# Two-layer diffusion trunk with eight experts: another order of the experts, another order inside a weight block, one list of leftover blocks

## The chip, the cores and the metric

The kernel runs on one core of one Trainium2 chip. The metric is the device time of one execution in microseconds (us); lower is better.

## What is computed

The reference is a trunk of two layers over 256 tokens of width 1024 in fp32 (layer 0: mLSTM and differential attention, then a dense SwiGLU; layer 1: a convolution module, then eight experts). The change touches the last sub-layer alone, each token's top two of eight experts:

```python
logits = (tokens @ router_w).astype(F32)
top_vals, top_idx = lax.top_k(logits, TOP_K)          # TOP_K = 2 of N_EXPERTS = 8
gates = jax.nn.softmax(top_vals, axis=-1)
...
def run_block(args):                                   # D = 1024, D_FF_EXPERT = 2816
    tok_idx, e = args
    xb = tokens[tok_idx]
    return (jax.nn.silu(xb @ w1[e]) * (xb @ w3[e])) @ w2[e]
```

An expert's three matrices are 3 x 1024 x 2816 fp32 numbers, 34.6 MB; eight experts are 277 MB, read from HBM in every execution.

## The kernel before, in words

All weights lie in HBM in units of 128 x 2048 fp32, one 1 MB (1.05 million bytes) transfer each. An expert is 33 units: its hidden width 2816 is cut into blocks j = 0 to 5 (five of 512 columns, one of 256), and a 512-wide block has two units of w1 (h = 0, 1: the two halves of the 1024 contraction rows), two of w3 and two of w2; the last block has one of each. The m1 and m3 units of one (j, h) are the "unit pair" of the change.

**Slots.** At run time the tokens that chose an expert are counted and gathered into slots. Expert 0 has FIRST = 96 slots. The other seven are ranked by their counts, and the rank of an expert gives it `SLOTS` = 128, 96, 96, 96, 64, 64 or 32 slots. `TURNS` (L37) is the order in which expert 0 (None) and the ranks take their turns, so before it is, in slots: 96, 64, 96, 96, 32, 128, 96, 64. With the given inputs the counts are 60 for expert 0 and 98, 82, 78, 70, 55, 51, 18 by rank, so no token is left over.

**Two kinds of expert.** The 128-slot expert (class `Expert`) splits each weight half into a high and a low part on ScalarE and VectorE (`half`, L363) and runs three passes with the full array. An expert with fewer slots (`few`, class `Tiled`, L1835) multiplies fp32 weights as they land. Its slots are cut into 64 (`wide`, L1848: column tiles of 64, m1 and m3 side by side in the array) and 32 (`narrow`, L1851: column tiles of 32, four side by side); 96 slots use both, 64 only wide, 32 only narrow. The profile shows wide matmuls as 128*64 and narrow ones as 128*32; each fp32 matmul is two records. `up2` (L1857) does one unit pair: the wide matmuls of its contraction tiles, then its narrow ones. `down2` (L1897) does one m2 unit in the same way. `act` (L1870) is silu times gate on ScalarE and VectorE, `turn` and `turned` (L1881, L1891) transpose the result on TensorE and copy it on VectorE for `down2`.

**The order.** The list `todo` (L2149 to L2182) holds the products in TensorE's order: for block j the pairs of (j, 0) and (j, 1), then the m2 units of block j - 1. `later(n, ...)` hangs small work before the n-th next product: `act` at once, `turn` after `wait` further products (L2164). TensorE, VectorE and ScalarE keep the order as written (`in_order`). The gathers of the next group of experts (`GROUPS`, L38) are hung into blocks 2 and 3 of the expert before it, an expert's way back to its tokens (`back`) into the first block of the next one. At the start of expert 0, `ranks` (L1966) counts, ranks and prepares the leftover bookkeeping on GpSimd and VectorE; its VectorE instructions stand before the `act` of block 0.

**The transfers.** SyncE issues all weight transfers, in the order in which `todo` uses the units; each waits until the buffer it writes is free, and all behind it wait too. The list `room` (L1557 to L1564) says which buffers the units take in turn: 6 "raw", 4 "w" (the rings of high and low parts, where no expert splits), 1 "gp", 4 "B8", so 15 ahead; around the 128-slot expert, which needs the rings itself, 6 + 1 + 3 = 10. `whole` (L1558) is the place of the 128-slot expert in `TURNS`, and the list is cut by it: the cycles of 15 run up to 30 units before that expert, the cycles of 10 until 8 units behind it. Counted through the list, the last 11 units of the kernel before take three "w" buffers (253 to 255 of 0 to 263), three "B8" (256 to 258) and five "raw". "B8" has seven buffers; the output sum `acc` and the two parts of the tokens keep three, and the two parts of the sum (`sums_`, L2028) take two more from block 3 of the last expert on.

**Leftovers.** After the experts, `overflow` (L2043) would run experts again for tokens that found no slot: two numbers are loaded into registers of every engine, and two `If` blocks with a loop over all eight experts (`block`, L2055, written out in each) and a third `If` are passed. With these inputs all are jumped over.

Of the kernel before, what the change touches and what calls it, by code (L numbers as in the profile page):

```python
# [19 lines left out]
P = 128  # L20
# [13 lines left out]
FIRST = 96  # L34

SLOTS = (128, 96, 96, 96, 64, 64, 32)
TURNS = (None, 4, 1, 2, 6, 0, 3, 5)  # L37
GROUPS = ((0,), (1, 2), (3, 4), (5,), (6, 7))  # L38
NV = 2

# [196 lines left out]
def build(ctx: ExitStack, tc: tile.TileContext, d, unit, dbg=None):  # L237
# [1463 lines left out]
    def few(i):  # L1701
        return slots_of(i) < P
# [132 lines left out]
    class Tiled(Expert):  # L1835
# [21 lines left out]
        def up2(self, j, h, ws):  # L1857

            w_ = 512 if j < 5 else 256
            if h == 0:  # L1860
                self.pp = self.banks("mm")
            (x,), nk = self.x(), UW // w_
            for on, fn, o, s in ((self.A, self.wide, self.oa, 64), (self.B, self.narrow, self.ob, 32)):
                for k in range(nk if on else 0):
                    kk = nk * h + k
                    for n, w in enumerate(ws):
                        w = w[k // (nk // 2)].rearrange("p (k c) -> p k c", c=w_)[:, k % (nk // 2)]
                        fn(self.pp, x[:, kk, o : o + s], n, w, kk == 0, kk == KT - 1)

        def act(self, j):  # L1870
            w_ = 512 if j < 5 else 256
# [25 lines left out]
        def down2(self, j, h, w):  # L1897

            nf = 4 if j < 5 else 2
            if self.yp is None:  # L1900
                self.yp = self.banks("aux")
            t = self.hhl[j]
            for on, fn, o, s in ((self.A, self.wide, 0, 64), (self.B, self.narrow, 64 * nf * self.A, 32)):
                for k in range(2 if on else 0):
                    q = 2 * h + k
                    m = 64 * q if s == 64 else 64 * (q % (nf // 2)) + 32 * (q // (nf // 2))
                    for c in range(2):
                        fn(self.yp, t[:, o + m : o + m + s], c, w[k][:, 512 * c : 512 * c + 512], j + q == 0, j == 5 and q == 1)

        def parts(self, g=None):  # L1910

# [38 lines left out]
    bases = tl([P, NE - 1], "bases", I32)  # L1950

    posv, selv, gtv = (tl([P, TT, 2 * NE], n) for n in ("posv", "selv", "gtv"))
    cmi = tl([P, 2], "cmi", I32)

    def by_rank(dst, src):

# [9 lines left out]
    def ranks():  # L1966

        pcnt = pm("aux")
        for t in range(TT):
            mm(pcnt[:, 0:8], one, sel[:, t, :], t == 0, t == TT - 1)  # L1970
        cnt, key = tl([P, NE], "cnt"), tl([P, NE], "key")
        A.copy(cnt, pcnt[:, 0:8])

        G.tensor_scalar(key, cnt, float(NE), None, ALU.mult)
        G.tensor_tensor(key, key, K("iota8"), ALU.subtract)
        sq = [P, NE - 1, NE - 1]
        V.tensor_tensor(r7[0], key[:, 1:].unsqueeze(1).to_broadcast(sq), key[:, 1:].unsqueeze(2).to_broadcast(sq), ALU.is_gt)
        rank = tl([P, NE - 1], "rank")
        V.tensor_reduce(rank, r7[0], AX.X, ALU.add)
        i7 = K("iota8")[:, : NE - 1]  # L1980
        V.tensor_tensor(r7[1], rank.unsqueeze(1).to_broadcast(sq), i7.unsqueeze(2).to_broadcast(sq), ALU.is_equal)
        x = tl(sq, "r7", bufs=4)
        G.tensor_tensor(x, r7[1], K("iota8")[:, 1:].unsqueeze(1).to_broadcast(sq), ALU.mult)
        b = tl([P, NE - 1], "bf")
        V.tensor_reduce(b, x, AX.X, ALU.add)
        V.tensor_scalar(bases, b, float(NU), None, ALU.mult)
        by_rank(posr, pos)
        by_rank(selr, sel)

        cap = tl([P, NE], "cap")  # L1990
        G.memset(cap, float(FIRST))
        G.memset(cap[:, 1:], float(P))
        for r in range(1, NE - 1):
            if SLOTS[r] != SLOTS[r - 1]:
                x = tl([P, NE - 1], "capx", bufs=2)
                V.tensor_scalar(x, rank, float(r), float(SLOTS[r - 1] - SLOTS[r]), ALU.is_ge, ALU.mult)
                G.tensor_tensor(cap[:, 1:], cap[:, 1:], x, ALU.subtract)
        for n in range(2):
            c = slice(NE * n, NE * n + NE)
            for t in range(TT):  # L2000
                if n == 0:
                    G.tensor_tensor(posv[:, t, c], pos[:, t], cap, ALU.subtract)
                G.tensor_copy(selv[:, t, c], sel[:, t])
                G.tensor_copy(gtv[:, t, c], gt[:, t])
            G.tensor_tensor(cnt, cnt, cap, ALU.subtract)
            V.tensor_reduce(key[:, n : n + 1], cnt, AX.X, ALU.max)
            if n == 0:
                G.memset(cap, float(P))
        for t in range(TT):
            G.tensor_tensor(posv[:, t, NE:], posv[:, t, :NE], cap, ALU.subtract)  # L2010
        V.tensor_scalar(cmi, key[:, 0:2], 0.0, None, ALU.max)

    base = []

# [26 lines left out]
        return d["w"][bass.ds(base + unit[key], 1)].rearrange("o p c -> p (o c)")  # L2041

    def overflow():  # L2043
        over = [nc.values_load(cmi[0:1, n : n + 1], min_val=0, max_val=T) for n in range(2)]

        for n in range(2):
            with tc.If(over[n] > 0):  # L2047
                with tc.For_i(0, NE, 1) as e:
                    block(e, e + NE * n)
        with tc.If(over[0] > 0):  # L2050
            for t in range(TT):
                for c in range(2):
                    acc_parts(t, c)

    def block(e, q):  # L2055

        colv = tl([P, 3, TT], "ovc")
        for n, src in enumerate((posv, selv, gtv)):
# [10 lines left out]
        gather([O2[:, t, :] for t in range(TT)], [(0, P, g2)], bank="mm")  # L2069

        def load(n, j, h):
            return halves(raw(None, unit_from(e * NU, (n, 0, j, h))))

        x2 = Expert(lambda: g2, lambda w: OT2, lambda t: colv[:, 2, t : t + 1], bank="mm")
        for j in range(6):
# [73 lines left out]
    for i in range(NE):  # L2149
# [6 lines left out]
        for j in range(6):  # L2156
            for h in range(2 if j < 5 else 1):
                if few(i):
                    todo.append(([("m1", i, j, h), ("m3", i, j, h)], None, partial(x.up2, j, h)))
                else:  # L2160
                    for n in ("m1", "m3"):
                        for q in range(2):
                            todo.append(([(n, i, j, h)], q, partial(x.up, j, h, int(n == "m3"), q)))
            wait = 1 if few(i) else 2 if (i, j) == (last, 5) else 3  # L2164
            later(0, partial(x.act, j))
            later(wait, partial(x.turn, j), partial(x.turned, j))
            if (i, j) == (last, 1):
                later(2, row)
            if (i, j) == (last, 3):
                later(1, slot_gate, *[partial(acc_parts, t, c) for t in range(TT) for c in range(2)])  # L2170
            g = group_of.get(i + 1)
            if g is not None and g != group_of[i]:
                if j == 2:
                    later(0, partial(new_group, g), *[lambda g=g, t=t: groups[g].onehot(t) for t in range(TT)])
                    later(3, lambda g=g: groups[g].turn())
                if j == 3:
                    later(1, *[lambda g=g, k=k: groups[g].gather((k,)) for k in range(4)])
            if j:
                downs(i, j - 1)
            elif i:  # L2180
                downs(i - 1, 5)
# [104 lines left out]
```

## Time and profile before

| | us |
|---|---|
| median of 3 runs | 1334.69 (1329.05 to 1337.04) |
| the profiled execution | 1333.75 |
| its span, first to last instruction | 1331.9 |
| TensorE busy in the span | 1262.3 |
| expert 0 starts / the last product of the last expert ends | 603.0 / 1310.0 |
| units of weights read by the experts | 264 |

Times of rows are counted from the start of the span; what lies around the span is 1.85 us. "PE" is TensorE, "PEld" its weight loads, "DVE" VectorE, "ACT" ScalarE, "POOL" GpSimd, "SP" SyncE. A name with q (SPq, PEldq) is the engine's sequencer, which handles branches, semaphores and the issuing of transfers. The granted clock is 1.00 at 2.4 GHz and 0.50 at 1.2 GHz; a figure between is a mean over the stretch. A busy TensorE isn't one at its peak: the records of matmuls that run side by side overlap.

### The profile page before, as it was taken

The page shows a single profiled execution, that of the slowest core. Times are in us where ns is not written, and L with a number is a line of the kernel's source. Part 1 is how long each engine was busy: PE and PEld are TensorE (multiplying, and loading weights), DVE is VectorE, ACT ScalarE, POOL GpSimd, SP SyncE. Part 2 cuts the span into 40 slices and gives each one's busy share as a digit, 9 for nine tenths or more (in the row PEclk, how much of TensorE's full clock was granted, in tenths as well). Part 3 has the DMA queues.
Part 4 walks back from the last instruction along what each step waited for, and adds up shares of the span by engine and source line. Part 5 has one row for each costly group of instructions (what it writes and reads, how often), then busy time and mean ns, then how long its engine had stood idle before and what let it go on. Part 6 is the DMA issues. An engine that isn't in the chain of part 4 may idle for free. (4 is left out here: it accounts for less than half of the span.)

```text
span 1331.9 us, 22705 instructions
## 1 busy us (share of the span) xinstructions
PE 1262.3 (95%) x9256; PEld 799.1 (60%) x9256; DVE 630.6 (47%) x1040; ACT 430.3 (32%) x785; POOL 31.3 (2%) x78
## 2 busy tenths in 40 slices
PE   7999999899999998999999999999986999999994
PEld 5878777799998886684343333433443778434332
DVE  4689758698877667752101112011121888211122
ACT  4553346564434553342020000210002678100111
POOL 1000001100000000001000000000000000000000
PEclk9999999999999998888999999999999999999997
DMA  8728820478987626788789999998989999799963
GB/s 334 288 100 297 310 91 25 163 319 345 375 315 293 221 104 175 236 306 318 265 331 399 418 418 416 414 380 323 369 339 420 420 419 362 305 417 381 407 252 138
DMA packets 70808, 406.48 MB, mean 305 GB/s; under 512 B 7842, under 2 KB 12194, under 8 KB 31268
## 3 DMA queue, kind: packets, MB, share of 16 engines
q1 hardware_dynamic: 70692, 404.91, 78.6%
q8 instruction: 76, 1.25, 0.4%
q14 instruction: 40, 0.33, 0.1%
HBM read 402.94 MB, written 1.93 MB: 304 GB/s over the span
## 5 line engine op out<-in xcount | busy, mean ns | idle before, releaser
L373 DVE TENSOR_TENSOR wlo<-raw,whi 128x1024 fp32r<-128x1024 f32 x150 | 180.9, 1223 | 51.5 <-ACT whi L372 51.0
L282 PE MATMUL mm<-raw,gL 128*32 128x256 f32 (+3 forms) x1432 | 193.8, 441 | 7.9 <-DMA raw<-w 6.3
L372 ACT CAST whi<-raw 128x1024 fp32r<-128x1024 f32 x150 | 154.9, 1051 | 92.4 <-PE mm L282 59.1
L282 PE MATMUL mm<-B,whi 128*128 128x256 f32 x960 | 169.8, 280 | 0.2 <-DVE B L632 0.2
L1878 DVE TENSOR_TENSOR cv<-cv,mm 64x512 f32<-64x512 f32 (+1 forms) x36 | 23.3, 647 | 284.2 <-ACT cv L1877 283.9
L282 PEld LDWEIGHTS mm<-B,whi 128*128 128x128 f32 x960 | 147.5, 189 | 2.3 <-PE mm L282 0.6
L282 PEld LDWEIGHTS mm<-raw,gL 128*32 128x32 f32 (+1 forms) x1432 | 75.1, 121 | 105.6 <-issue 74.6
L282 PE MATMUL mm<-B,wlo 128*128 128x256 f32 x480 | 134.0, 279 | 0.0
L1877 ACT ACTIVATE cv<-mm 64x512 f32<-64x512 f32 (+1 forms) x36 | 19.9, 553 | 351.2 <-PE mm L282 351.1
L282 PE MATMUL mm<-B,gL 128*32 128x256 f32 (+3 forms) x736 | 112.0, 442 | 2.5 <-DMA B<-w 2.5
L282 PE MATMUL aux<-whi,pT 128*128 128x512 f32 (+2 forms) x392 | 104.1, 437 | 0.0
L282 PEld LDWEIGHTS mm<-B,wlo 128*128 128x128 f32 x480 | 90.4, 188 | 0.0
L282 PE MATMUL aux<-raw,pT 128*32 128x256 f32 (+1 forms) x632 | 79.0, 459 | 1.3 <-DVE cvt L1878 0.7
L282 PE MATMUL aux<-wlo,pT 128*128 128x512 f32 (+2 forms) x276 | 71.4, 442 | 1.1 <-DVE wlo L373 1.1
L282 PEld LDWEIGHTS mm<-B,gL 128*32 128x32 f32 (+1 forms) x736 | 41.5, 120 | 46.4 <-issue 33.8
L282 PEld LDWEIGHTS aux<-whi,pT 128*128 128x128 f32 (+2 forms) x392 | 49.0, 160 | 25.8 <-issue 14.7
L282 PE MATMUL mm<-U,whi 128*128 128x256 f32 (+1 forms) x240 | 64.3, 330 | 0.0
L282 PE MATMUL mm<-whi,B 128*128 128x512 f32 (+1 forms) x192 | 60.1, 389 | 2.9 <-ACT whi L372 2.9
L282 PE MATMUL aux<-B,pT 128*32 128x256 f32 (+2 forms) x392 | 58.6, 468 | 2.9 <-SPq L2047 2.9
L282 PE MATMUL mm<-whi,gL 128*32 128x256 f32 (+3 forms) x360 | 57.5, 443 | 0.0
L282 PE MATMUL mm<-wlo,gL 128*32 128x256 f32 (+3 forms) x360 | 56.2, 436 | 0.0
L282 PE MATMUL mm<-U,wlo 128*128 128x256 f32 (+1 forms) x160 | 52.4, 328 | 0.0
(454 smaller groups left out, 1836.5 us busy)
## 6 DMA issues: line engine op xcount, KB each, us to landing
raw<-w SPq DMA_DIRECT2D x239, 1024.0 KB, 7.3
B<-w SPq DMA_DIRECT2D x69, 1024.0 KB, 11.4
whi<-w SPq DMA_DIRECT2D x52, 512.0 KB, 8.5
wlo<-w SPq DMA_DIRECT2D x52, 512.0 KB, 9.0
gp<-w SPq DMA_DIRECT2D x16, 512.0 KB, 9.8
m<-w SPq DMA_DIRECT2D x16, 512.0 KB, 10.0
B<-hd SPq DMA_DIRECT2D x24, 142.0 KB, 5.2
x<-x SPq DMA_DIRECT2D x2, 512.0 KB, 4.7
```

The lines of the kernel that those rows point to most:

```text
L282: PE.matmul(out, lhsT, rhs, start=start, stop=stop)
L372: A.copy(hi, rq)
L373: V.tensor_tensor(lo, rq, f(hi), ALU.subtract)
L1877: A.activation(s, p_[:64, :w], AF.Silu)
L1878: V.tensor_tensor(s, s, p_[64:, :w], ALU.mult)
```

## The change

`TURNS` gives 96, 32, 96, 96, 64, 96, 128, 64 slots: the 32-slot expert comes second, the 128-slot expert seventh. `up2` and `down2` of an expert with both kinds of tiles run the wide matmuls of (j, 0) and of (j, 1) first and hold the narrow ones of both until then. `turn` of a few-slot expert comes one product later, but for block 0 of expert 0 and the last block of the last expert. `ranks` makes a list of at most eight leftover blocks (expert, place, count), and `overflow` runs one loop over that list under one `If`.

```diff
@@ -34,7 +34,7 @@
 FIRST = 96
 
 SLOTS = (128, 96, 96, 96, 64, 64, 32)
-TURNS = (None, 4, 1, 2, 6, 0, 3, 5)
+TURNS = (None, 6, 1, 2, 4, 3, 0, 5)
 GROUPS = ((0,), (1, 2), (3, 4), (5,), (6, 7))
 NV = 2
 
@@ -1858,14 +1858,23 @@
 
             w_ = 512 if j < 5 else 256
             if h == 0:
-                self.pp = self.banks("mm")
+                self.pp, self.held = self.banks("mm"), []
             (x,), nk = self.x(), UW // w_
-            for on, fn, o, s in ((self.A, self.wide, self.oa, 64), (self.B, self.narrow, self.ob, 32)):
-                for k in range(nk if on else 0):
-                    kk = nk * h + k
-                    for n, w in enumerate(ws):
-                        w = w[k // (nk // 2)].rearrange("p (k c) -> p k c", c=w_)[:, k % (nk // 2)]
-                        fn(self.pp, x[:, kk, o : o + s], n, w, kk == 0, kk == KT - 1)
+            ws = [[w[k // (nk // 2)].rearrange("p (k c) -> p k c", c=w_)[:, k % (nk // 2)] for w in ws] for k in range(nk)]
+
+            def go(fn, kk, w, o, s):
+                for n in range(2):
+                    fn(self.pp, x[:, kk, o : o + s], n, w[n], kk == 0, kk == KT - 1)
+
+            for k, w in enumerate(ws):
+                if self.A:
+                    go(self.wide, nk * h + k, w, self.oa, 64)
+                if self.B:
+                    self.held.append((nk * h + k, w))
+            if not self.A or nk * h + nk == KT:
+                for kk, w in self.held:
+                    go(self.narrow, kk, w, self.ob, 32)
+                self.held = []
 
         def act(self, j):
             w_ = 512 if j < 5 else 256
@@ -1899,13 +1908,24 @@
             nf = 4 if j < 5 else 2
             if self.yp is None:
                 self.yp = self.banks("aux")
-            t = self.hhl[j]
-            for on, fn, o, s in ((self.A, self.wide, 0, 64), (self.B, self.narrow, 64 * nf * self.A, 32)):
-                for k in range(2 if on else 0):
-                    q = 2 * h + k
-                    m = 64 * q if s == 64 else 64 * (q % (nf // 2)) + 32 * (q // (nf // 2))
-                    for c in range(2):
-                        fn(self.yp, t[:, o + m : o + m + s], c, w[k][:, 512 * c : 512 * c + 512], j + q == 0, j == 5 and q == 1)
+            if h == 0:
+                self.held = []
+            t, o = self.hhl[j], 64 * nf * self.A
+
+            def go(fn, q, w, m, s):
+                for c in range(2):
+                    fn(self.yp, t[:, m : m + s], c, w[:, 512 * c : 512 * c + 512], j + q == 0, j == 5 and q == 1)
+
+            for k in range(2):
+                q = 2 * h + k
+                if self.A:
+                    go(self.wide, q, w[k], 64 * q, 64)
+                if self.B:
+                    self.held.append((q, w[k], o + 64 * (q % (nf // 2)) + 32 * (q // (nf // 2))))
+            if not self.A or 2 * h + 2 == nf:
+                for q, w, m in self.held:
+                    go(self.narrow, q, w, m, 32)
+                self.held = []
 
         def parts(self, g=None):
 
@@ -1950,7 +1970,7 @@
     bases = tl([P, NE - 1], "bases", I32)
 
     posv, selv, gtv = (tl([P, TT, 2 * NE], n) for n in ("posv", "selv", "gtv"))
-    cmi = tl([P, 2], "cmi", I32)
+    blocks = tl([P, 3, 8], "blocks", I32)
 
     def by_rank(dst, src):
 
@@ -1995,20 +2015,32 @@
                 x = tl([P, NE - 1], "capx", bufs=2)
                 V.tensor_scalar(x, rank, float(r), float(SLOTS[r - 1] - SLOTS[r]), ALU.is_ge, ALU.mult)
                 G.tensor_tensor(cap[:, 1:], cap[:, 1:], x, ALU.subtract)
+        more = tl([P, 2 * NE], "more")
         for n in range(2):
             c = slice(NE * n, NE * n + NE)
             for t in range(TT):
-                if n == 0:
-                    G.tensor_tensor(posv[:, t, c], pos[:, t], cap, ALU.subtract)
+                G.tensor_tensor(posv[:, t, c], pos[:, t] if n == 0 else posv[:, t, :NE], cap, ALU.subtract)
                 G.tensor_copy(selv[:, t, c], sel[:, t])
                 G.tensor_copy(gtv[:, t, c], gt[:, t])
             G.tensor_tensor(cnt, cnt, cap, ALU.subtract)
-            V.tensor_reduce(key[:, n : n + 1], cnt, AX.X, ALU.max)
+            G.tensor_scalar(more[:, c], cnt, float(2 * NE), None, ALU.mult)
+            G.tensor_tensor(more[:, c], more[:, c], K("iota8"), ALU.subtract)
             if n == 0:
                 G.memset(cap, float(P))
-        for t in range(TT):
-            G.tensor_tensor(posv[:, t, NE:], posv[:, t, :NE], cap, ALU.subtract)
-        V.tensor_scalar(cmi, key[:, 0:2], 0.0, None, ALU.max)
+            else:
+                G.tensor_scalar(more[:, c], more[:, c], float(NE), None, ALU.subtract)
+
+        top, ti = tl([P, 8], "top"), tl([P, 8], "ti", U32)
+        V.max(top, more)
+        V.max_index(ti, top, more)
+        V.tensor_copy(key, ti)
+        V.tensor_copy(blocks[:, 0], key)
+        V.tensor_scalar(cnt, key, float(NE), float(NE), ALU.is_ge, ALU.mult)
+        V.tensor_tensor(key, key, cnt, ALU.subtract)
+        V.tensor_scalar(blocks[:, 1], key, float(NU), None, ALU.mult)
+        V.tensor_scalar(top, top, 0.0, None, ALU.is_gt)
+        V.tensor_reduce(key[:, 0:1], top, AX.X, ALU.add)
+        V.tensor_copy(blocks[:, 2, 0:1], key[:, 0:1])
 
     base = []
 
@@ -2041,18 +2073,18 @@
         return d["w"][bass.ds(base + unit[key], 1)].rearrange("o p c -> p (o c)")
 
     def overflow():
-        over = [nc.values_load(cmi[0:1, n : n + 1], min_val=0, max_val=T) for n in range(2)]
-
-        for n in range(2):
-            with tc.If(over[n] > 0):
-                with tc.For_i(0, NE, 1) as e:
-                    block(e, e + NE * n)
-        with tc.If(over[0] > 0):
+
+        n = nc.values_load(blocks[0:1, 2, 0:1], min_val=0, max_val=NE)
+        with tc.If(n > 0):
+            with tc.For_i(0, n, 1) as i:
+                q = nc.values_load(blocks[0:1, 0, bass.ds(i, 1)], min_val=0, max_val=2 * NE - 1)
+                at = nc.values_load(blocks[0:1, 1, bass.ds(i, 1)], engines=(ET.SP,), min_val=0, max_val=(NE - 1) * NU)
+                block(at, q)
             for t in range(TT):
                 for c in range(2):
                     acc_parts(t, c)
 
-    def block(e, q):
+    def block(at, q):
 
         colv = tl([P, 3, TT], "ovc")
         for n, src in enumerate((posv, selv, gtv)):
@@ -2069,7 +2101,7 @@
         gather([O2[:, t, :] for t in range(TT)], [(0, P, g2)], bank="mm")
 
         def load(n, j, h):
-            return halves(raw(None, unit_from(e * NU, (n, 0, j, h))))
+            return halves(raw(None, unit_from(at, (n, 0, j, h))))
 
         x2 = Expert(lambda: g2, lambda w: OT2, lambda t: colv[:, 2, t : t + 1], bank="mm")
         for j in range(6):
@@ -2161,7 +2193,7 @@
                     for n in ("m1", "m3"):
                         for q in range(2):
                             todo.append(([(n, i, j, h)], q, partial(x.up, j, h, int(n == "m3"), q)))
-            wait = 1 if few(i) else 2 if (i, j) == (last, 5) else 3
+            wait = 2 if (i, j) == (last, 5) and not few(i) else 1 if (i, j) in ((0, 0), (last, 5)) else 2 if few(i) else 3
             later(0, partial(x.act, j))
             later(wait, partial(x.turn, j), partial(x.turned, j))
             if (i, j) == (last, 1):
```

## Rows read from the trace of the kernel before

**Rows 1.** Stretches, one per expert; busy us of each engine, clock, DMA share, GB/s

```profile
core 0: us, PE busy (x) PEld busy (x) DVE busy (x) ACT busy (x) POOL busy (x), PEclk, DMA share, GB/s
603.00:703.10 100.10, 99.47 (x896) 41.27 (x895) 15.20 (x50) 15.76 (x37) 4.46 (x23) 0.98 0.83 304
703.10:768.50 65.40, 65.40 (x338) 23.96 (x336) 10.78 (x19) 4.85 (x9) 0.00 (x0) 1.00 1.01 410
768.50:869.10 100.60, 100.60 (x905) 41.22 (x901) 14.51 (x29) 11.96 (x31) 0.00 (x0) 1.00 1.02 416
...
967.40:1030.60 63.20, 48.11 (x633) 25.48 (x625) 10.65 (x24) 9.96 (x24) 0.00 (x0) 0.96 0.97 388
1030.60:1136.30 105.70, 104.34 (x492) 82.28 (x492) 88.00 (x89) 77.62 (x97) 0.00 (x0) 0.97 0.99 400
...
1233.70:1310.00 76.30, 71.51 (x358) 26.14 (x354) 13.37 (x23) 8.44 (x16) 0.00 (x0) 0.98 0.80 328
```

**Rows 2.** Stretches, the ends of expert 0 and of the fourth expert, same columns

```profile
680.00:703.10 23.10, 23.10 (x253) 10.76 (x249) 2.67 (x6) 3.02 (x9) 0.00 (x0) 1.00 0.95 356
...
960.00:969.00 9.00, 9.00 (x141) 4.44 (x135) 1.07 (x3) 0.35 (x2) 0.00 (x0) 1.00 0.51 183
```

**Rows 3.** Timeline of PE, a 96-slot block: start us, us, records, [idle before <-releaser]

```profile
1193.31 0.64 PE L282 MATMUL mm<-whi,gL 128*64 128x512 f32 x1
...
1196.90 0.41 PE L282 MATMUL mm<-whi,gL 128*32 128x256 f32 x2
...
1198.76 2.94 PE L282 MATMUL aux<-B,pT 128*64 128x512 f32 x24
1201.63 0.46 PE L1887 MATMUL aux<-cst,cv 64*128 64x64 f32 x4
```

**Rows 4.** Timeline of PE, two unit pairs at 32 slots, then at 64 slots

```profile
967.42 0.39 PE L282 MATMUL mm<-whi,gL 128*32 128x256 f32 x2
...
970.99 2.94 PE L282 MATMUL aux<-B,pT 128*64 128x512 f32 x24
...
1271.60 7.04 PE L282 MATMUL mm<-raw,gL 128*64 128x512 f32 x32
1278.47 1.89 PE L282 MATMUL aux<-raw,pT 128*64 128x512 f32 x8
```

**Rows 5.** Timelines of PE, DVE and POOL where ranks runs

```profile
616.49 5.52 PE L282 MATMUL mm<-raw,gL 128*64 128x512 f32 x48
622.63 0.46 PE L1887 MATMUL aux<-cst,cv 64*128 64x64 f32 x4 [0.63 <-DVE cv L1878]
...
621.49 0.16 DVE L2006 TENSOR_REDUCE key<-cnt 128x1 f32<-128x8 f32 x1 [0.60 <-POOL cnt L2005]
...
621.89 0.69 DVE L1878 TENSOR_TENSOR cv<-cv,mm 64x512 f32<-64x512 f32 x1
...
621.26 0.20 POOL L2005 TENSOR_TENSOR cnt<-cnt,cap 128x8 f32<-128x8 f32 x1
```

**Rows 6.** The stretch of the 128-slot gather, its one-hot products (tile oh) alone

```profile
993.40:1016.70 23.30, 4.98 (x34) 4.19 (x34) 0.00 (x0) 0.00 (x0) 0.93 1.01 417
```

**Rows 7.** The end of the last expert: SP's issues, PE's timeline, a stretch

```profile
1266.78 23.61 SPq L347 DMA_DIRECT2D B<-w  x3
...
1294.99 3.06 PE L282 MATMUL aux<-B,pT 128*64 128x512 f32 x8 [2.86 <-SPq L2047]
...
1300.51 3.45 PE L282 MATMUL mm<-raw,gL 128*64 128x256 f32 x29 [1.63 <-SPq L2047]
...
1292.00:1300.50 8.50, 4.02 (x13) 0.99 (x10) 0.53 (x2) 0.00 (x0) 0.00 (x0) 0.80 1.00 420
```

**Rows 8.** The jump over the leftovers: PE's timeline, its sequencer's branches (ns, min/median/max)

```profile
1317.56 3.75 PE L282 MATMUL mm<-B,identr 128*128 128x512 f32 x8 [7.60 <-PEq L2047]
...
L2047 PEldq COMPARE_BRANCH  x2: 3464/3826/4187, 1308.7 to 1312.7; - x2
...
L2050 PEldq COMPARE_BRANCH  x1: 254/254/254, 1317.1 to 1317.1; - x1
```

## Prediction

> **What bounds the kernel now.** I read the stretches by expert first, since only the experts' stage and the end behind it are touched. One unit is 1.0486 MB; at the 420 GB/s that the transfers reach when nothing holds them [rows 7] a unit takes 2.50 us and an expert's 33 units 82.4 us. Against that stands TensorE. A 96-slot expert takes 100.6 us with no idle TensorE [rows 1]: TensorE bounds it, and the transfers run ahead. The 64-slot one takes 65.4 us, also without idle [rows 1]: it lives on units loaded ahead. The 32-slot one takes 63.2 us with TensorE busy 48.1 and the clock at 0.96 [rows 1]: it waits for transfers. The last expert takes 76.3 us at 0.80 DMA share [rows 1], with waits that the timeline shows singly. So two things count: TensorE's time in the four 96-slot experts, and how many units lie ready ("lead") where a quick expert begins. I then read the timelines of one block of each kind, of ranks, and of the end.
>
> **Term 1, the narrow products held back.** In a 512-wide block a unit pair takes 5.45 us (1193.31 to 1198.76) and an m2 unit 2.87 (1198.76 to 1201.63) [rows 3]. Two pairs and two m2 units: 10.90 and 5.74. After the change both pairs' wide products follow each other, then both pairs' narrow ones. The wide run is that of the 64-slot expert, 6.87 us (1271.60 to 1278.47), the narrow run that of the 32-slot expert, 3.57 us (967.42 to 970.99) [rows 4]; the sum is 10.44, so 0.46 goes. For m2, 16 steps of wide cost 6.87/16 = 0.429 and of narrow 0.223; an m2 unit is 4 of each, 2.61 us, and shows 2.87, so 0.26 is the cost of starting its two runs. Two units start four runs now, two after: 0.26 less. Together 0.72 a block. Blocks of this kind are five in each of four experts (the 256-wide one has a single pair): 20 x 0.72 = **14.4 us**. Lower bound the first part alone, 9.2; upper bound both starts of m2 gone, 20 x 0.98 = 19.6. It counts in full only where TensorE is the bound, as in rows 1. `act` then starts behind a longer narrow run, but its transposes come a product later too, with the m2 units of the block before (5.4 us) ahead of them; `act` on both engines and both parts is under 2 us (0.69 for the largest of its instructions [rows 5]), so this costs nothing. The held units give their buffers back some 5 us later; I put that at nothing as long as there is lead, and price it below.
>
> **Term 2, the list of leftover blocks.** ranks stands on VectorE ahead of the `act` of block 0, and `turn` of block 0 keeps its early place. Today its last GpSimd result comes at 621.46, two VectorE instructions follow 0.2 apart, the silu product starts at 621.89, and TensorE waits 0.63 us before transposes at 622.63 [rows 5]. After: five more GpSimd instructions (two products and three subtractions) stand before the last result, about 0.25 each by that 0.20: +1.2, so 622.7. Then VectorE has eleven instructions at 0.2 each, to 624.9; it is 3.0 us later than now, less 0.3 for the shorter run before it, and the transposes come at about 625.4. TensorE however is there sooner: of the pair it does in between, only the wide products (half of 6.87, 3.5 us) remain, the narrow ones are held. It starts that pair at some 616.2 instead of 616.49 [rows 5] and is done at 619.7. So it waits 5.7 us instead of 0.63: **+5.1**. The held narrow work isn't lost, it only can't fill this hole. In the end stretch two waits of 2.86 and 1.63 us went with a mean clock of 0.80 over 8.5 us [rows 7], which is 3.4 us at 1.2 GHz and 1.7 us of work lost; for a wait of 5.7 us I add **+2**. Nothing hides it: expert 0 is bound by TensorE and all buffers ahead are full. Bounds: 0 (GpSimd's work done in earlier gaps) to +9.
>
> The Trainium skill ("TensorE: Matmul & The Clock Gate", section "HAM oscillation — how this bites in real kernels") says that a TensorE left waiting falls to half rate and pays again when it resumes, which speaks against this part of the change. The trace agrees in the 0.80 above. By the rule the wait costs more than its length; without it term 2 would be 5.1.
>
> **Term 3, 32 slots second.** Before, the expert takes 63.2 us at 388 GB/s [rows 1]: 24.5 MB, 23.4 units. It needs its own 33 and two of the next, so its lead was 11 to 12: the cycle of 10 buffers plus what was in use. It was as full as it could be: in the 9 us before, the transfers ran at 183 GB/s [rows 2], with no buffer free. After, the cycle of 15 reigns there. At the end of expert 0 the transfers run at 356 GB/s, 0.95 share [rows 2], so about 16 are issued and 3 of them still on the way: lead 13. Then 35 - 13 = 22 units x 2.50 = 55 us. The next expert has 96 slots and needs two pairs of units before its first narrow product: 5.0 us of transfer against 3.5 of wide products, twice, 3 us. 58 against 63.2: -5.2. But the gather for the 128-slot expert, 4.98 us of TensorE [rows 6], lay inside that wait; now the third group's gather stands in the fifth expert, where TensorE has no wait: +5.0. And the 128-slot expert began starved, with a clock of 0.97 over 105.7 us [rows 1], 3.2 us of work lost; at a 96-slot start paced by transfers about 1 is lost: -2.2. Net **-2.4**. Bounds: +5 (the lead no larger, the gather paid) to -12 (all 16 landed, 19 units).
> Then the lead: 96-slot experts take about 97 us after term 1 against 82.4, so each adds 14 us or 6 units; the fifth (64 slots, 65.4 + 5) takes 12 us from it, the sixth gives it back, the 128-slot one (about 98) fills it. No other expert should wait.
>
> **Term 4, the buffers at the end.** SyncE issues three B8 transfers from 1266.78 over 23.61 us [rows 7]: the third finds no buffer, since the parts of the sum have taken two, and the five behind it stand in the queue. That stretch ends with waits of 2.86 and 1.63 us and the lost 1.7 [rows 7]: 6.2 us. After, counting the list, the last units are 6 raw (242 to 247), 4 w, 3 B8 (252 to 254), 9 raw: the B8 ones are asked for before the sum's parts. Of the nine, 255 to 260 reuse buffers of block 2 and 3, and only 261 to 263 wait for block 4's second pair; TensorE still has an m2 unit (1.8) and the last pair (3.5) and transposes ahead of them, as long as two units take. I leave 1.2 of wait: **-5**, bounds -6.2 and 0.
>
> **Term 5, the jump.** TensorE idles 7.60 us between last expert and sum; its two long branches take 3464 and 4187 ns, the third 254 [rows 8]. One `If` and one load stay. One long branch, the short one and a load go: **-4.5**; bounds -3.5 (the long one left is the slower, and its load no sooner) and -7.3 (none left).
>
> **Sum.** -14.4 + 7.1 - 2.4 - 5 - 4.5 = -19.2. From the profiled execution, 1333.75 (span 1331.9 and 1.85 around it): 1314.5. That execution is 0.94 under the median of the runs, so against 1334.69 I say 1315.
>
> **Rivals.**
> A. Starting a run costs nothing, the 0.46 belongs to other differences of those experts: term 1 gone, 1315 + 14.4 = 1329. For: the rows come from different experts. Against: in one block 5.45 is above 8 steps of each kind, 5.21.
> B. The list stands in no one's way: term 2 gone, 1315 - 7 = 1308. For: GpSimd is nearly idle, its copies ran early. Against: the eleven VectorE instructions alone are 2 us, and the hole in TensorE's order remains.
> C. Order and buffers give nothing: terms 3 and 4 gone, 1315 + 7.4 = 1322. For: the gather's price is as large as the gain in lead.
> D. Slower: the held pairs starve the next experts. Before, a first pair's narrow run (5.45 less 3.5) filled the time until the second pair; held back, it leaves 5.0 - 3.5 = 1.5 us of wait in each block that starts with less than two pairs ready. If that goes on through the 15 blocks of the third, fourth and sixth expert it costs 22, and the fifth, entered without lead, takes 82.4 instead of 70: 1315 + 22 + 12 = 1349. It decides from some 5 units of lead at the fifth expert's start. Against: those experts take 97 us of TensorE for 82.4 us of transfers, so lead must grow.
>
> **How the numbers follow.** Forecast 0.5, A 0.12, B 0.15, C 0.18, D 0.05. The range takes in A and B and the bounds of term 3: 1303 to 1330; beyond it lie D and the far ends of A and B. A measurement of this kernel can tell about 1% (13.3 us) from no change: below 1321.3 lie most of the forecast (0.43), B (0.15) and under half of C (0.08), so faster 0.66; slower over 1%, beyond 1348, is half of D and a rest, 0.04; same 0.30.
>
> **What would show it.** Right: wide records in runs of 6.9 us in the 96-slot experts and narrow runs of 3.6; TensorE idle 5 to 6 us near 620 with VectorE L1878 as releaser; the second expert about 58 us at 420 GB/s; no 20 us hole in SyncE's issues near the end; one long branch and a gap near 3 us before the sum. Wrong: a 96-slot block still near 17 us, waits for transfers in the third or fourth expert, or a DMA share under 0.9 in the second.

## The result, and the profile after

The changed kernel takes 1322.0 us (median of 7 runs, 1319.89 to 1324.35) against 1337.04 for the kernel before on the same chip: ratio 0.9899, 95% interval 0.9878 to 0.9919, so 1.0% faster. The forecast was 1315, the range 1303 to 1330. The profiled execution of after took 1319.89 (span 1317.9), 13.9 us under that of before; the forecast for this difference was 19.2.

The stretches of after, one per expert, with the columns of [rows 1]:

```profile
601.70:706.30 104.60, 99.34 (x900) 43.40 (x899) 15.93 (x57) 15.55 (x37) 5.52 (x28) 0.95 0.73 280
706.30:763.20 56.90, 45.53 (x597) 23.50 (x596) 8.98 (x20) 3.68 (x9) 0.00 (x0) 0.88 1.01 421
763.20:865.60 102.40, 101.10 (x911) 44.02 (x911) 14.43 (x29) 12.54 (x32) 0.00 (x0) 0.98 1.02 420
865.60:962.00 96.40, 96.40 (x893) 40.70 (x891) 13.93 (x25) 6.99 (x15) 0.00 (x0) 1.00 0.95 381
962.00:1033.00 71.00, 71.00 (x371) 28.08 (x370) 12.05 (x23) 8.45 (x18) 0.00 (x0) 1.00 1.02 420
1033.00:1131.70 98.70, 98.70 (x904) 42.93 (x902) 19.92 (x35) 17.66 (x38) 0.00 (x0) 1.00 0.87 352
1131.70:1232.20 100.50, 100.50 (x471) 78.28 (x470) 84.21 (x81) 70.38 (x77) 0.00 (x0) 1.00 0.96 370
1232.20:1301.20 69.00, 68.31 (x335) 26.92 (x334) 15.45 (x24) 8.93 (x17) 0.00 (x0) 1.00 0.93 378
```

Set against before by the expert's kind: expert 0 is 4.5 us longer (104.6 for 100.1), the 32-slot one 6.3 shorter (56.9 for 63.2), the three later 96-slot ones go from 100.6, 98.3 and 97.4 to 102.4, 96.4 and 98.7, the 64-slot one from 65.4 to 71.0, the 128-slot one from 105.7 to 100.5, the last from 76.3 to 69.0. The stage is 7.4 shorter, the idle time before the sum 4.6, the sum 0.6, and the stage began 1.3 earlier: 13.9. (Starts of this stage lie between 599.7 and 606.8 in the profiles of this study, whatever the kernel, so the 1.3 isn't the change's.) The largest gain of the forecast, four 96-slot experts quicker by 3.6 each, is the one that is mostly missing.

**Why expert 0 is longer.** Timelines of PE and DVE where ranks ends, and the stretch behind, in after:

```profile
614.87 3.65 PE L282 MATMUL mm<-raw,gL 128*64 128x512 f32 x16
623.79 0.69 PE L1896 MATMUL aux<-cst,cv 64*128 64x64 f32 x4 [5.26 <-DVE cv L1887]
...
621.20 0.18 DVE L2034 MAX8 top<-more 128x8 f32<-128x16 f32 x1 [3.05 <-POOL more L2031]
...
623.04 0.69 DVE L1887 TENSOR_TENSOR cv<-cv,mm 64x512 f32<-64x512 f32 x1
...
624.60:630.20 5.60, 5.60 (x17) 1.52 (x16) 0.00 (x0) 0.00 (x0) 0.00 (x0) 0.63 0.02 3
```

TensorE finishes the wide run at 618.5 and waits 5.26 us, where [rows 5] show 0.63. DVE got GpSimd's result at 621.20, spent 1.8 us on the list, and only then began the product that the transposes need. Then TensorE works on at a granted clock of 0.63: the wait costs more than its length.

**What the runs of tiles became.** PE's timeline of an unbroken block of after:

```profile
917.57 1.94 PE L282 MATMUL mm<-whi,gL 128*64 128x512 f32 x8
...
924.59 1.07 PE L282 MATMUL mm<-whi,gL 128*32 128x256 f32 x16
...
928.18 5.52 PE L282 MATMUL aux<-B,pT 128*64 128x512 f32 x48
933.62 0.46 PE L1896 MATMUL aux<-cst,cv 64*128 64x64 f32 x4
```

Two pairs take 10.61 us (917.57 to 928.18) for 10.90, two m2 units 5.44 for 5.74: 0.59 a block, where the forecast had 0.72. Others of the same expert look like this:

```profile
879.09 3.65 PE L282 MATMUL mm<-B,gL 128*64 128x512 f32 x16
882.67 0.46 PE L1896 MATMUL aux<-cst,cv 64*128 64x64 f32 x4
...
883.19 7.24 PE L282 MATMUL mm<-B,gL 128*64 128x512 f32 x80
890.37 1.94 PE L282 MATMUL aux<-raw,pT 128*64 128x512 f32 x8
892.23 1.19 PE L282 MATMUL aux<-xn,oht 64*128 64x512 f32 x4
893.35 3.80 PE L282 MATMUL aux<-raw,pT 128*64 128x512 f32 x40
...
898.13 0.40 PE L1896 MATMUL aux<-cst,cv 64*128 64x64 f32 x4
...
898.59 3.65 PE L282 MATMUL mm<-raw,gL 128*64 128x512 f32 x16
902.17 1.20 PE L282 MATMUL aux<-xn,oht 64*128 64x512 f32 x4
903.30 7.25 PE L282 MATMUL mm<-raw,gL 128*64 128x512 f32 x80
```

Between the two wide products stands other work: `turn` at 882.67 (it comes a product later, and in block 1 that is amid the pairs), the way back (tile xn) at 892.23 and 902.17. Such a pair takes 3.58 and 7.18, 10.76 without what stands between: 0.14 saved, not 0.29. The same places of the kernel before:

```profile
894.30 2.94 PE L282 MATMUL aux<-raw,pT 128*64 128x512 f32 x24
897.17 0.50 PE L282 MATMUL aux<-xn,oht 64*128 64x512 f32 x1
897.18 0.46 PE L1887 MATMUL aux<-cst,cv 64*128 64x64 f32 x4
...
898.30 2.94 PE L282 MATMUL aux<-raw,pT 128*64 128x512 f32 x24
...
902.29 5.52 PE L282 MATMUL mm<-raw,gL 128*64 128x512 f32 x48
```

There `turn` and the way back started within 0.01 us of each other and ran side by side. The stretch of that m2 pair took 7.99 us (894.30 to 902.29) and takes 8.22 (890.37 to 898.59): a loss of 0.23. The fourth expert adds up: pairs 3 x 0.29 + 2 x 0.14, m2 4 x 0.29 - 0.23, together 2.1 against 1.9 measured (98.3 to 96.4).

**The rest of after**: PE at the start of the third expert; SyncE's issues near the end; PE before the sum, and its long branch:

```profile
763.18 1.04 PE L282 MATMUL mm<-raw,gL 128*64 128x512 f32 x2 [1.25 <-DMA raw<-w]
765.52 5.20 PE L282 MATMUL mm<-raw,gL 128*64 128x512 f32 x16 [1.30 <-DMA raw<-w]
...
774.08 2.14 PE L282 MATMUL mm<-raw,gL 128*32 128x256 f32 x34
...
1259.72 3.03 SPq L347 DMA_DIRECT2D B<-w  x3
1263.72 25.50 SPq L347 DMA_DIRECT2D raw<-w  x9
...
1304.23 3.46 PE L282 MATMUL mm<-B,identr 128*128 128x512 f32 x8 [3.00 <-PEq L2078]
...
L2078 PEldq COMPARE_BRANCH  x1: 3852/3852/3852, 1299.9 to 1299.9; - x1
```

The first wide run after the quick expert takes 10.9 us (763.18 to 774.08) instead of 7.0, and TensorE waits 1.25 us for transfers before it and 1.30 in it: waits in the third expert were one of the forecast's signs of being wrong. The B8 transfers now go out in 3.0 us instead of 23.6 [rows 7]; of the nine raw ones behind them the last three come after a gap of 14.6 us (1272.5 to 1287.2), as term 4 had it for these three. One long branch is left of two, and the idle time before the sum is 3.00 for 7.60 [rows 8].

### The profile page after: what moved, and what is told of

It reads as the page before. It is cut to its first block, busy times and chain, and to the rows that moved or that the text cites. A ratio compares the mean times of both kernels' runs of the same rounds, so it can differ in the third digit from the quotient of the medians.

```text
span 1317.9 us, 22697 instructions
## 1 busy us (share of the span) xinstructions
PE 1254.1 (95%) x9256; PEld 807.2 (61%) x9256; DVE 633.0 (48%) x1049; ACT 431.2 (33%) x784; POOL 32.4 (2%) x83
## 5 line engine op out<-in xcount | busy, mean ns | idle before, releaser
L373 DVE TENSOR_TENSOR wlo<-raw,whi 128x1024 fp32r<-128x1024 f32 x154 | 186.0, 1222 | 47.6 <-ACT whi L372 46.5
L372 ACT CAST whi<-raw 128x1024 fp32r<-128x1024 f32 x154 | 159.4, 1048 | 102.6 <-PE mm L282 64.3
L282 PE MATMUL mm<-B,gL 128*32 128x256 f32 (+3 forms) x808 | 124.4, 449 | 3.3 <-DMA B<-w 3.3
L282 PEld LDWEIGHTS mm<-raw,gL 128*32 128x32 f32 (+1 forms) x1392 | 77.9, 122 | 80.8 <-issue 57.5
L282 PE MATMUL aux<-whi,pT 128*128 128x512 f32 (+2 forms) x400 | 100.9, 425 | 0.6 <-DMA whi<-w 0.6
L282 PEld LDWEIGHTS mm<-B,gL 128*32 128x32 f32 (+1 forms) x808 | 46.7, 123 | 55.3 <-issue 40.8
L282 PE MATMUL aux<-wlo,pT 128*32 128x256 f32 (+2 forms) x284 | 69.1, 429 | 1.9 <-DVE wlo L373 1.1
L1903 DVE COPY pT<-aux 128x384 f32<-128x384 f32 (+4 forms) x42 | 19.0, 453 | 107.8 <-PE aux L1896 99.1
## 6 DMA issues: line engine op xcount, KB each, us to landing
wlo<-w SPq DMA_DIRECT2D x52, 512.0 KB, 10.9
```

The lines of the kernel that those rows point to most:

```text
L282: PE.matmul(out, lhsT, rhs, start=start, stop=stop)
L372: A.copy(hi, rq)
L373: V.tensor_tensor(lo, rq, f(hi), ALU.subtract)
L1903: V.tensor_copy(h[:, :o], pt[:, :o])
```

## Experiments

The first four share the runs of the kernel before; e5 to e8 and e9 to e11 do likewise.

**e1_merge.** The held narrow products alone: the hunks of `up2`, `down2` and `wait` on the kernel before.

```diff
+            if not self.A or nk * h + nk == KT:
+                for kk, w in self.held:
+                    go(self.narrow, kk, w, self.ob, 32)
```

> The kernel before with the held narrow products (and the later turn) alone. Theory: each of the 20 wide-and-narrow blocks loses the starts of two to three runs, 0.4 to 0.6 us, some 10 us; since only the wide products of the pair beside ranks are left there, TensorE waits about 2 us more in block 0 of expert 0. Sum -8 us against the kernel before, and the 32-slot expert still takes about 63 us. Rival 1, starting a run costs nothing: no change beyond the +2 us. Rival 2, held pairs starve the next products: slower by 5 us or more, with TensorE waiting for transfers in the third, fourth and seventh expert.

Measured: 1329.37, ratio 0.9961 (0.9946 to 0.9976), 5.9 us under before's median where 8 were forecast. The fourth and the seventh expert, and the wait in expert 0:

```profile
866.60:963.00 96.40, 96.40 (x893) 40.69 (x891) 13.93 (x25) 7.00 (x15) 0.00 (x0) 1.00 0.93 365
...
1131.10:1225.80 94.70, 94.70 (x872) 40.53 (x871) 15.56 (x25) 7.65 (x16) 0.00 (x0) 1.00 0.91 365
...
620.05 0.46 PE L1896 MATMUL aux<-cst,cv 64*128 64x64 f32 x4 [2.49 <-DVE cv L1887]
```

Where no idle TensorE confuses it, a 96-slot expert gains 1.7 (the third), 1.9 and 2.8 us, about 2 where 3.6 was forecast. Expert 0 loses 1.1: even without the list the narrow work is missing from the wait for ranks, which is 2.49 instead of 0.63.

**e2_list.** The list alone: the hunks of `ranks`, `overflow` and `block` on the kernel before.

```diff
+        n = nc.values_load(blocks[0:1, 2, 0:1], min_val=0, max_val=NE)
+        with tc.If(n > 0):
+            with tc.For_i(0, n, 1) as i:
```

> The kernel before with the list of leftover blocks alone (ranks and overflow). Theory: the chain on GpSimd and VectorE is 2.8 us longer, the wait of 0.63 us in block 0 becomes 3.4 us, maybe with 1 to 2 us of half clock behind it; the jump before the sum falls from 7.6 to 3.0 us. Sum between -2 and 0 us. Rival, only the jump counts because the chain is hidden: -4.6 us. Rival, the chain costs as much as in the changed kernel whatever the order of products: +2 us.

Measured: 1332.37, ratio 0.9977 (0.9967 to 0.9987): slightly faster.

```profile
605.10:711.80 106.70, 103.31 (x898) 42.33 (x897) 16.28 (x58) 15.76 (x37) 5.52 (x28) 0.94 0.77 282
...
628.57 0.69 PE L1887 MATMUL aux<-cst,cv 64*128 64x64 f32 x4 [3.39 <-DVE cv L1878]
1320.27 3.59 PE L282 MATMUL mm<-B,identr 128*128 128x512 f32 x8 [2.67 <-PEq L2058]
```

The list opens a wait of 3.39 us in expert 0 and takes 4.9 from the one before the sum (2.67 for 7.60). What it costs in expert 0 stays open: this profile, of the longest of the twelve runs, shows 6.6 more there, of which some 1.1 is a low clock that it brought from the stage before; the medians are 2.9 apart, which leaves about 2.0 for it.

**e3_order.** The order alone, on the kernel before; the cut of `room` follows `whole`.

```diff
-TURNS = (None, 4, 1, 2, 6, 0, 3, 5)
+TURNS = (None, 6, 1, 2, 4, 3, 0, 5)
```

> The kernel before with the new order of experts alone. Theory: the wait in the last expert (6.2 us) goes, and the 32-slot expert with the start of the next one takes 61 us for 63.2 plus 3.2, while the third group's gather of 5 us comes to lie in the open: sum -5 to -8 us, nearly all of it from the last expert. Rival, the order itself gives the gain: the stretch from the 32-slot expert's start to the next one's second block is over 10 us shorter. Rival, neither gives anything: within 2 us of before.

Measured: 1325.60, ratio 0.9934 (0.9918 to 0.9950), 9.7 us by the medians where 5 to 8 were forecast. The second, third and last expert:

```profile
699.60:755.40 55.80, 44.31 (x601) 21.97 (x592) 8.57 (x19) 3.69 (x9) 0.00 (x0) 0.89 1.01 408
755.40:858.50 103.10, 102.63 (x911) 41.91 (x911) 14.78 (x30) 12.57 (x32) 0.00 (x0) 0.98 1.02 416
...
1229.50:1298.90 69.40, 68.78 (x335) 25.91 (x334) 15.53 (x24) 9.00 (x17) 0.00 (x0) 1.00 0.93 374
```

By kind against before: expert 0 -0.2, 32 slots -7.4, third +2.5, fourth +0.1, 64 slots +5.6 (a gather now stands in it), the 96-slot one behind it +3.5 (it now holds the gather for the last two experts), 128 slots -5.1, last -6.9. Without the last expert this is -0.9: the order moves waiting about, and the end gains.

**e4_late.** After, with the VectorE part of the list hung further behind, clear of block 0's `act`.

```diff
+    def listed():
+        more, cnt, key = late[0]
...
             later(3, first)
+            later(6, listed)
```

> The changed kernel with the eleven VectorE instructions of the list put behind the act of block 1 of expert 0; nothing else moved. Theory: the wait of 5.3 us near 620 falls to about 0.6 and the half clock behind it goes: 6 to 7 us faster than the changed kernel, all of it in expert 0. Rival, expert 0's time is given back in the second expert, since transfers bound that one: no change against the changed kernel, the second expert 5 to 7 us longer.

Measured: 1315.58, ratio 0.9847 (0.9829 to 0.9865), 0.5% under after's. Expert 0:

```profile
604.60:701.90 97.30, 96.91 (x900) 42.73 (x901) 15.91 (x57) 15.54 (x37) 5.51 (x28) 0.99 0.78 299
```

Expert 0 is 7.3 us shorter than in after; TensorE's wait there is 0.39. The second expert takes 57.0 (56.9 in after), so nothing is given back there. So the list's place, not the list, cost what term 2 said. Against e3_order, which differs by the held products and the list, the four 96-slot experts gain 2.6, 0.7, 2.0 and 2.3: 7.6 in all.

**e5_split.** The opposite of the merge, on the kernel before: wide and narrow alternate with every contraction tile, 8 runs in a pair instead of 2 (16 in block 5's), 74 more in a 96-slot expert. The arithmetic is unchanged.

```diff
-            for on, fn, o, s in ((self.A, self.wide, self.oa, 64), (self.B, self.narrow, self.ob, 32)):
-                for k in range(nk if on else 0):
+            for k in range(nk):
+                for on, fn, o, s in ((self.A, self.wide, self.oa, 64), (self.B, self.narrow, self.ob, 32)):
```

> The kernel before with wide and narrow products of up2 alternating for every contraction tile: the same products, 8 runs in a pair instead of 2 (16 in the last block), 74 more runs in each of four experts. Theory, each change of tile shape costs 0.12 to 0.16 us: 9 to 12 us longer in each 96-slot expert, 35 to 47 us in all. Rival, what a merged pair saves belongs to the start of a product and not to the change of shape: within 5 us of before.

Measured: 1375.18, ratio 1.0315 (1.0292 to 1.0338). The second (64 slots, no narrow tiles) and the fourth expert:

```profile
712.30:777.70 65.40, 65.40 (x340) 23.99 (x338) 10.77 (x19) 4.85 (x9) 0.00 (x0) 1.00 1.00 404
...
888.90:997.90 109.00, 109.00 (x893) 31.92 (x893) 13.41 (x25) 7.00 (x15) 0.00 (x0) 1.00 0.84 311
```

The run takes 41.2 us more than before, as forecast. The 96-slot experts grow by 9.8, 10.7, 10.7 and 10.7, the 64-slot one by nothing, with as many instructions as before: 10.7/74 = 0.145 us for each change of tile shape. This also gives the two sizes seen in after: an unbroken pair of products makes two changes fewer (0.29), a broken one a single one fewer (0.14). The starts of the records in the fourth expert, here and in before, show where the time goes. From one wide product to the next it is 0.429 us, to a narrow one 0.529; from one narrow product to the next 0.216, to a wide one 0.329; the step behind a change is 0.05 (wide) or 0.025 (narrow) longer. That is 0.125 for one direction and 0.164 for the other, 0.145 on average. Where wide products go on to another PSUM bank without a change of shape, as from m1 and m3 to m2 in the 64-slot expert, the step stays 0.429 (709.62 to 710.05 in before), so it is the change of shape that costs. The seventh expert of e1_merge agrees: its records change shape 34 times for 53 in before, and it gains 2.8, 0.147 each. The Trainium skill ("TensorEngine Tiling (Array Packing)", section "Key Properties") says that a change of the tiling mode drains TensorE; the run agrees that a change has a price, and doesn't show what it is spent on.

**e6_tail.** Old order; three fewer B8 entries at the end of `room`, so that the last units take other buffers.

```diff
+    del room[-3:]
     xT_ = tl([P, KT, T], "B8")
```

> The kernel before with the last three B8 buffers taken off the list, so that the last eight units go to raw buffers; order of experts as before. Theory: the 20 us hole in the issues goes, the last expert takes 70 us for 76.2, sum -6 us. Rival, its last units come late whatever the buffers, since that expert starts with a lead of 12 and needs 33: under 2 us gained.

Measured: 1325.06, ratio 0.9935 (0.9920 to 0.9950).

```profile
1233.10:1302.40 69.30, 69.04 (x358) 25.74 (x354) 13.36 (x23) 8.44 (x16) 0.00 (x0) 1.00 0.89 358
```

The last expert takes 69.3 for 76.3, and the median is 8.9 under before's where 6 were forecast. This line gives what e3_order gives.

**e7_window.** Old order; one more cycle of 15 before the 128-slot expert, which also shifts the list's end.

```diff
-    while asked() < whole - 30:
+    while asked() < whole - 15:
```

> The kernel before with one more cycle of 15 buffers ahead of the 128-slot expert; order as before, 32 slots fifth. Theory, the buffers ahead and not the place decide what the 32-slot expert waits: it takes 53 to 57 us for 63.2, the rest as before, sum -6 to -10 us. Rival, the place decides: 62 to 64 us, no change.

Measured: 1323.24, ratio 0.9927 (0.9908 to 0.9947). The 32-slot expert in its old place, and the last expert:

```profile
965.60:1023.90 58.30, 49.10 (x633) 26.70 (x625) 10.65 (x24) 9.97 (x24) 0.00 (x0) 0.91 1.02 413
...
1227.70:1297.90 70.20, 69.46 (x358) 26.46 (x354) 13.36 (x23) 8.45 (x16) 0.00 (x0) 1.00 0.87 349
```

The 32-slot expert takes 58.3 for 63.2, a little over the forecast's 53 to 57: the cycle of 15 helps in the old place too, by 4.9 of the 7.4 that the new place shows in e3_order. The rest isn't as before: the list now ends in ten raw buffers without a B8, and the last expert takes 70.2 for 76.3, over half of the run's 10.7.

**e8_old_order** is e4_late with the old order and the edits of e6_tail and e7_window; **e9_buffers** is e8_old_order without the edit of e6_tail.

```diff
-TURNS = (None, 6, 1, 2, 4, 3, 0, 5)
+TURNS = (None, 4, 1, 2, 6, 0, 3, 5)
...
-    while asked() < whole - 30:
+    while asked() < whole - 15:
...
+    del room[-3:]
```

> The changed kernel with the list's VectorE instructions late, the order of experts of before, one more cycle of 15 and the last three B8 off the list. Theory, the gain of the new order was the buffers', and with the old order the 128-slot gather hides in the wait of the 32-slot expert: stage 681 to 686 us for 692.5 with the new order, so 1305 to 1310 us. Rival, the order has a gain of its own: at or above 1316 us.

> The run with the old order again, but with the last three B8 buffers left on the list (one more cycle of 15 moves the list's end, so that 13 raw buffers stand there). Theory: the last expert's 73 us in that run came of 16 raw buffers at the end, so it falls to 70 us; 1311 to 1313 us. Rival, the merged products themselves make the last stretch late: 73 us again, 1315 us.

Measured: e8_old_order 1314.89, 0.9862 (0.9843 to 0.9880); e9_buffers 1313.17, 0.9838 (0.9813 to 0.9864). The last expert of each:

```profile
1223.60:1296.60 73.00, 70.56 (x355) 28.02 (x354) 13.81 (x24) 8.38 (x16) 0.00 (x0) 1.00 0.87 350
```

```profile
1221.70:1292.00 70.30, 70.02 (x356) 26.87 (x354) 13.81 (x24) 8.45 (x16) 0.00 (x0) 1.00 0.89 364
```

e8_old_order missed its forecast and lies under its rival's time too: the two edits of `room` together leave too long a run of raw buffers at the end, and give back 2.7 us there, as e9_buffers shows. The old order with the list of buffers cut later is as quick as the new order (0.9838 against 0.9847 for e4_late).

**e10_unbroken** is e4_late with the way back, the gathers and the gathers' `turn` put off by a product where they would stand between two products of a pair, and a few-slot `turn` after one product at j = 0; **e11_best** is the same on e9_buffers.

```diff
+            fns = due.pop(i, [])
+            if second(i):
+                held_ = [fn for fn in fns if any(fn is g for g in free)]
+                due[i + 1] = held_ + due.get(i + 1, [])
```

> The changed kernel with the list's VectorE instructions late, and gathers, their transposes, the ways back and the transposes of block 0 moved out of the gap between the two products of a wide-and-narrow pair, to the next product. Theory: a pair that is broken by other work saves nothing, and some 18 of 40 are broken; each gains 0.29 us, 4 to 6 us against the run with the late list alone, in expert 0, the third, fourth and sixth. Rival, the missing half of the first term is the lesser saving of unbroken pairs alone: within 1 us.

> Both together: old order with one more cycle of 15, list late, pairs unbroken. Theory: 1306 to 1309 us, the fastest of all. Rival, with pairs unbroken the buffers come back later and the experts that wait take the gain: no faster than the better of the other two.

Measured: e10_unbroken 1314.92, 0.9851 (0.9831 to 0.9870); e11_best 1310.98, 0.9820 (0.9801 to 0.9840), the fastest kernel of the study. In e10_unbroken the fourth expert, the sixth, and a wait in it:

```profile
864.80:959.50 94.70, 93.87 (x891) 39.62 (x889) 13.75 (x25) 6.99 (x15) 0.00 (x0) 1.00 0.97 387
1030.40:1129.40 99.00, 96.74 (x904) 42.66 (x902) 19.74 (x35) 17.44 (x38) 0.00 (x0) 1.00 0.88 357
...
1098.49 1.14 PE L282 MATMUL aux<-oh,B 128*128 128x192 f32 x8 [1.42 <-ACT gL L1629]
```

Unbroken, the fourth expert gains another 1.7 (96.4 to 94.7). It then lies 3.6 under before, as term 1 had it for one expert, with 30 changes of shape for 52; by 0.145 each they make 3.2 of it. Expert 0 is 1.5 longer, nearly all of it a low clock that this execution brought from the stage before (0.66 over the first 8.2 us, 0.84 over 8.4 in e4_late). The sixth is 0.3 longer: work put off bunches, and TensorE waits for copies between its pieces (2.3 us idle). The 4 to 6 us of the forecast didn't come, and e10_unbroken can't be told from e4_late. e11_best, 2 us over its forecast, lies 2.2 under e9_buffers with intervals that overlap: whether keeping all pairs unbroken pays in sum stays open.

## Why the prediction was right and wrong

| | forecast | measured | from |
|---|---|---|---|
| term 1, held narrow products | -14.4 | -7.6 | 96-slot experts, e4_late less e3_order |
| term 2, place of the list | +7.1 | +7.3 | expert 0, after less e4_late |
| term 3, 32 slots second | -2.4 | -0.9 | e3_order without its last expert |
| term 4, buffers at the end | -5 | -6.9 | last expert, e3_order |
| term 5, the jump | -4.5 | -4.6 | idle time before the sum, after |

The sum is -12.7 where -19.2 was forecast. Term 1 alone fell 6.8 short; the others are off by 1.9 at most, and together by 0.3 to the other side. No term holds the 1.1 that the 32-slot expert lost (56.9 in after for 55.8 in e3_order); with 0.4 more gained in the last expert, 0.6 in the sum and 1.3 in the start of the stage, -12.7 becomes the -13.9 of the profiles. The time came to lie in the range although term 1, the largest, was worth half.

**Term 1 failed by size, in three steps.** "Together 0.72 a block" priced the start of a run at 0.23 for a pair and 0.13 for an m2 unit, by rows of other experts; e5_split gives 0.145 for both, so 0.58 a block. Over 20 blocks that is 2.8 of the 6.8. "Blocks of this kind are five in each of four experts" took all 80 of their starts to go. The records of PE, in order of start, change their tile shape 53, 55, 52 and 56 times in the four experts of e3_order and 37, 41, 35 and 41 times in e4_late: 62 fewer, since `turn`, the way back or a gather stands between the products of some pairs (e10_unbroken, which moves most of them, has 128 changes for these 154). The missing 18 are worth 2.6. In the fourth expert three of ten pairs are broken, and one of these also loses the overlap of the two, in sum 0.8 of 3.6. The last 1.4 lie, but for small differences in the others, in the third expert, which gains 0.7 where 14 changes fewer make 2.0: its start waits for transfers (rival D below). Note the bounds: I had 9.2 as the least, and the true value lies under it, since both bounds kept the count of 20. Rival A ("starting a run costs nothing") is refuted by e5_split, though its time, 1329, is about as far from 1322 as the forecast.

**Term 2 held.** The wait is 5.26 us for 5.7 forecast, its end 623.8 for 625.4, and the clock's part about 2; e4_late took all of it away, 7.3 us with the low clock behind the wait. e1_merge and e2_list show that each half makes a hole of 2.5 to 3.4 by itself. So rival B is refuted. The Trainium skill's rule ("TensorE: Matmul & The Clock Gate", section "HAM oscillation — how this bites in real kernels") that a TensorE left waiting starts again at half rate agrees with the 0.63 behind the wait: expert 0 paid 7.3 for 5.26.

**Term 3 was right by its net, with errors that cancel.** Its 58 us were 55 for the 32-slot expert and 3 for the start of the next one (the signs name them as the second expert's alone); e3_order has 55.8 and 2.5. The gather costs the 64-slot expert 5.6 (forecast 5.0). I left out that the gather of the last two experts moves from the 128-slot expert into the 96-slot one before it: +3.5, while the 128-slot one gains 5.1 for 2.2 forecast. e7_window shows that most of the 32-slot expert's gain is the buffers'.

**Term 4 held in its cause**, and at -6.9 lies past its bound of -6.2; the old order reaches it too (e6_tail). Rival C is refuted by e3_order, though its time, 1322, is the measured one: the right number would have come from the wrong cause.

**Rival D** shows in one place, the starved start of the third expert, and goes no further: the fourth to sixth have no idle TensorE. Most of it is the quick expert's: e3_order, without any held product, has the third expert 2.5 longer than before. But with held products it is 3.6 (102.4 in after for 98.8 in e1_merge), so 1.0 comes with them. The 1.1 of the 32-slot expert may be theirs too: it starts with about a unit less (421 GB/s over 56.9 us are 22.8 units, 408 over 55.8 in e3_order 21.7). The prediction put the later return of the held buffers "at nothing as long as there is lead"; these two experts begin with little, and some 2 us are lost there. No run tells the late buffers from the rest of what was held.

## What to carry to other kernels

A merge of runs saves by the number of shape changes that really go, so count them in TensorE's written order with all the small work that stands between, not in the loop that is edited. A longer chain on a slow engine ahead of a critical instruction is free only while TensorE has work in hand; the same edit that regroups TensorE's work may be what removes that cover. Where a new order seems to gain, see what moved with it: here a cut in the list of buffers gave as much without any new order.

## What the runs showed of the hardware that was not expected

- Alternating 64- and 32-column tiles cost 0.145 us per change with no idle TensorE in the rows: it hides in busy time (109.0 us busy of 109.0 in e5_split's fourth expert).
- Two products of the same 64*128 tile shape from different helpers, the transposes and the way back, started 0.01 us apart and overlapped (1.13 us for both, from 897.17 in before); set apart in after, they take 1.12 (from 892.23) and 0.46 (from 898.13).
- One busy buffer cost much: the three B8 issues took 23.6 us [rows 7] and take 3.0 in after, with five more transfers behind them in the queue; other buffers there gave 6.9 us of the last expert (e6_tail), though its transfers showed 0.80 busy [rows 1].
